# Block sums made in place for two weight matrices, norm sums in two row buffers, and one product moved, in a two-layer encoder step

## The chip, the cores and the metric

The kernel runs on one core of one Trainium2 chip. The metric is the device time of one execution in microseconds; three runs of the kernel before the change gave a median of 2988.94 us (2987.65 to 2989.17). PE is TensorE, DVE VectorE, ACT ScalarE, POOL GpSimd, SP the engine that issues the DMAs.

## The reference, cut to what matters

The step has two layers over 1024 prompt tokens and 8 x 16 sample tokens, 1152 columns in all, with 1024 features. Layer 0 mixes by forgetting attention, layer 1 by sliding-window attention. What the change touches is the part of each layer behind the attention:

```python
        h = h + _rms(mix, norm_mix_post[i])
        f = _swiglu(_rms(h, norm_ffn_pre[i]), ffn_w_gate[i], ffn_w_up[i], ffn_w_down[i])
        h = h + _rms(f, norm_ffn_post[i])
        gate = jax.nn.sigmoid(_rms(h, ple_norm[i]) @ ple_w_gate[i] + ple_b_gate[i])
        h = h + gate * (p[i] @ ple_w_proj[i])
```

with `_rms(x, g) = x * rsqrt(mean(x*x) + EPS) * g` over the features and `_swiglu(a, ...) = (silu(a @ w_gate) * (a @ w_up)) @ w_down`; the hidden width is 2816 = 22 x 128. All data are float32.

## The kernel before, in words

Activations lie with features on the partitions, in three column blocks of 384 columns: cC, cA and cB. A float32 product is made of three fp32r matmuls: each operand is split into a rounded high part (`round_r`, an ACT copy, L139) and the rest (`low_part`, a DVE subtraction, L145); `mm3` (L215 to L217) multiplies high by high, high by low and low by high.

`layer_tail` does everything behind the attention: output projection, residual and norms, SwiGLU, down projection, gate. Its steps are entered with `plan.add` and `plan.tile`; `Plan.run` then lists them: it keeps a planned clock for each of PE, ACT, DVE and LOAD (DMA issues on SP), takes at each turn the step that can start first (ties by due time), and calls it, so the order of the instructions on each engine is that in which the planner calls them. A step states its planned cost, the steps that it waits for, and which buffers it takes and frees; the dictionary in the `Plan(...)` call at L1085 says how many of each there are: one `acc`, two `sq`, two `y`, six product banks `mm`.

A norm (`plan_rms`, from L350) squares the eight feature tiles of a column block in four ACT activations of 768 columns. The first goes into `acc`, the others into `sq`; DVE adds them to `acc` (L365, 768 wide) and at last its two halves (L367). PE sums over the partitions (`total`, tile `pstat`, L233), DVE takes the root (`rsqrt`, 12 operations of 3 columns, L241 to L247), PE spreads it (`spread`, `prms`, L254), ACT copies it into a row `rr` (L380). For each block the output projection is followed by a norm, the residual (L424, L428; loads of the old h on SP, L420), a second norm and its gain products (`normed`, L1195).

The gate and up projections are computed by a Strassen-Winograd scheme on blocks: columns cA and cB against pairs of 128 hidden columns, feature halves against each other. The left operands are `Y11`, `Y21`, `Y22` and the differences `T1` to `T4` (`minus`, L1229, and `operand`, L139 and L145), made in the two `y` buffers which hold the mixer's blocks. The weight blocks are A and B, the two loaded 128x1024 pieces x1 and x2, and two sums, C and D, built on DVE by `s_sum` (L1315) from the halves X1 and X2 in a buffer of tag `y`. `matrix(g, up)` enters one weight matrix (11 groups g, gate and up): loads, splits (`parts_of`), seven half products of 12 matmuls into banks X, Y and Z, and the plain products of cC (`plain`, 24 matmuls, two halves). Bank X is used several times: Y11's product is copied out (`copied("11")`), T2 is added on top, copied (`"21"`, by ACT at L1353 for gate, by DVE at L1355 for up), then T1 is added on top, and so on. The first two matrices, (0, 0) and (0, 1), are `EARLY`: their plain products are made ahead (`when=0`), and they are loaded a second time for the Strassen products.

During the Strassen stage of layer 0 and 1 the weights of the gate stage are split as well (`presplit`, L1463 to L1478, through `st` and `sq`). The down projection (`kstep`) reads rows back from DRAM (`h_load`, L1529) and weights (`wd_load`, L1506).

Of the kernel before, what the change touches and what calls it, by code (L numbers as in the profile page):

```python
# [10 lines left out]
F32 = mybir.dt.float32  # L11
# [7 lines left out]
P = 128  # L19
D = 1024  # L20
KT = 8
# [67 lines left out]
def tile_kernel(ctx: ExitStack, tc: tile.TileContext, i, o, upto=99):  # L89
# [260 lines left out]
    def plan_rms(plan, src, after, out="rr", slot=None, ready=()):  # L350


        box = {}

        def square(k):
            if k:
                box[k] = t = tp.tile([P, 2, C], F32, name="sq", tag="sq", bufs=NSQ)
            else:
                box["acc"] = t = tp.tile([P, 2, C], F32, name="acc", tag="acc", bufs=1)
            nc.scalar.activation(t, src()[:, 2 * k:2 * k + 2, :], AF.Square)  # L360

        def gather(k):
            acc = box["acc"]
            if k < 4:
                nc.vector.tensor_tensor(acc, acc, box.pop(k), ADD)  # L365
            else:
                nc.vector.tensor_tensor(acc[:, 0], acc[:, 0], acc[:, 1], ADD)  # L367

        def sums():
            box["ps"] = total(box["acc"][:, 0])  # L370
# [11 lines left out]
        last = begin = plan.add(ACT, 0.735, step(square, 0), after[0], takes=["acc"])  # L382
        for k in range(1, 4):
            box["read"] = s = plan.add(ACT, 0.735, step(square, k), after[k] + [begin], takes=["sq"])
            last = plan.add(DVE, 0.87, step(gather, k), [s, last], frees=["sq"])
        last = plan.add(DVE, 0.47, step(gather, 4), [last])
# [679 lines left out]
    def layer_tail(l, oc, Wo, oa0, order, specs_kv=(), more=None):  # L1066
# [18 lines left out]
        plan = Plan(act=4 + (len(oa0[1]) == KT), raw=1, w0=2, w1=3, acc=1, sq=NSQ, rr=NRR, st=2, mm=6, hs=STB, row=NROW, y=2)  # L1085
# [204 lines left out]
        def matrix(g, up, when=1):  # L1290
# [58 lines left out]
            def copied(n, bank, eng=ACT):  # L1349

                def fn():
                    if eng == ACT:
                        nc.scalar.copy(put_row(temp(n)), ps(bank))  # L1353
                    else:
                        nc.vector.tensor_copy(put_row(temp(n)), ps(bank))  # L1355
                add(eng, 0.37 if eng == ACT else 0.47, fn, r=[(m, "ps", bank)], w=[(g, temp(n))], takes=["row"], **soon())
# [30 lines left out]

            whole = ("A", x1, [(m, "x", 0)]), ("B", x2, [(m, "x", 1)])
# [11 lines left out]
            wa = tags[m][0] if early else parts_of(m, *whole[0])  # L1400
            add(DVE, 0.6, step(s_sum, 1), r=[(m, "x", 1)], w=[(m, "s1")], takes=["y"])
# [6 lines left out]
            wb = tags[m][1] if early else parts_of(m, *whole[1])  # L1408
# [4 lines left out]
            if not early:  # L1413
                plain(0, "A", [])
                plain_out(0)
# [3 lines left out]
            product("X", "C", 1, "T2")  # L1419
            copied("21", "X", DVE if up else ACT)  # L1420
# [5 lines left out]
            if not early:  # L1426
                plain(1, "B", [])
                plain_out(1)
# [6 lines left out]
            if up:  # L1435
                diff("u11", "r12", "r11")
                store("r11", t_d[0, g], ("t", 0, g))
                diff("r12", "r22", "r12")
                diff("u22", "r22", "u11")
                store("u11", t_d[3, g], ("t", 3, g))  # L1440
                store("r22", t_d[2, g], ("t", 2, g))
                store("r12", t_d[5, g], ("t", 5, g))
                diff("u21", "r21", "u22")
                store("u22", t_d[4, g], ("t", 4, g))
                store("r21", t_d[1, g], ("t", 1, g))
                store("u21", t_d[6, g], ("t", 6, g))
# [61 lines left out]
        for half in range(2):  # L1508
            for f in range(FFT):
                last_load[0] = add(LOAD, 0.75, step(wd_load, f, half), w=[("W", f, half)], after=[last_load[0], marks[-2]],  # L1510
                                   takes=["act"] if half == 0 and f % 3 == 0 else [])

        def kstep(wsrc, wkey, hsrc, hkey, new, start, stop, evict):
# [24 lines left out]
            x = add(LOAD, 0.85, h_load, r=[hkey], after=last_row, takes=["row", "row"])  # L1538
# [708 lines left out]
```

## Time and profile before

| What | us |
|---|---|
| median of three runs | 2988.94 |
| the profiled execution | 2988.7 |
| its span | 2986.9 |
| PE busy in it | 2873.0 |
| DVE busy | 1894.1 |
| ACT busy | 1279.5 |

The span runs from the first to the last instruction on the chip; the execution's own time holds 1.8 us beside it. [...] A wait is given as the engine, the operation that waited, the one that released it, the total, how often, and the longest.

### The profile page before, as it was taken

The page shows a single profiled execution, that of the slowest core. Times are in us where ns is not written, and L with a number is a line of the kernel's source. Part 1 is how long each engine was busy: PE and PEld are TensorE (multiplying, and loading weights), DVE is VectorE, ACT ScalarE, POOL GpSimd, SP SyncE. Part 2 cuts the span into 40 slices and gives each one's busy share as a digit, 9 for nine tenths or more (in the row PEclk, how much of TensorE's full clock was granted, in tenths as well). Part 3 has the DMA queues.
Part 4 walks back from the last instruction along what each step waited for, and adds up shares of the span by engine and source line. Part 5 has one row for each costly group of instructions (what it writes and reads, how often), then busy time and mean ns, then how long its engine had stood idle before and what let it go on. Part 6 is the DMA issues. An engine that isn't in the chain of part 4 may idle for free. (4 is left out here: it accounts for less than half of the span.)

```text
span 2986.9 us, 48188 instructions
## 1 busy us (share of the span) xinstructions
PE 2873.0 (96%) x17564; PEld 2753.4 (92%) x17564; DVE 1894.1 (63%) x4187; ACT 1279.5 (43%) x2652; POOL 198.0 (7%) x324
## 2 busy tenths in 40 slices
PE   8999999998799999999999999998799999999999
PEld 8999877798699999999999988898799999999999
DVE  6253477767766656558878436658755555459875
ACT  6222266654433333345544245744433333255542
POOL 0000155400000000000000022200000000000000
PEclk9999999999799999999999999999899999999999
DMA  7364577534144444563365667344233333553364
GB/s 257 106 201 144 166 191 196 135 121 130 68 154 153 156 160 161 174 216 93 113 211 191 204 201 225 113 142 130 75 122 115 112 116 114 174 163 105 102 210 147
DMA packets 307041, 453.15 MB, mean 152 GB/s; under 512 B 40002, under 2 KB 253380, under 8 KB 306772
## 3 DMA queue, kind: packets, MB, share of 16 engines
q1 hardware_dynamic: 306804, 450.08, 47.9%
q8 instruction: 138, 2.26, 0.3%
q14 instruction: 99, 0.81, 0.1%
HBM read 315.60 MB, written 136.20 MB: 151 GB/s over the span
## 5 line engine op out<-in xcount | busy, mean ns | idle before, releaser
L215 PE MATMUL ps<-ahi,whi 128*128 128x384 f32 x1008 | 343.6, 341 | 0.7 <-ACT ev L589 0.7
L217 PE MATMUL ps<-ahi,wlo 128*128 128x384 f32 x1008 | 340.1, 337 | 0.2 <-DMA wlo<-wpg_d 0.2
L216 PE MATMUL ps<-alo,whi 128*128 128x384 f32 x1008 | 339.9, 337 | 0.0
L215 PE MATMUL pd<-row,whi 128*128 128x384 f32 x968 | 330.5, 341 | 9.5 <-ACT row L139 9.5
L216 PE MATMUL pd<-row,whi 128*128 128x384 f32 x968 | 329.8, 341 | 0.7 <-DVE row L145 0.7
L217 PE MATMUL pd<-row,wlo 128*128 128x384 f32 x968 | 328.5, 339 | 0.0
L215 PE MATMUL ps<-chi,whi 128*128 128x384 f32 x704 | 235.5, 335 | 0.0
L217 PE MATMUL ps<-chi,wlo 128*128 128x384 f32 x704 | 235.2, 334 | 0.0
L216 PE MATMUL ps<-clo,whi 128*128 128x384 f32 x704 | 235.2, 334 | 0.0
L145 DVE TENSOR_TENSOR wlo<-wraw,whi 128x1024 fp32r<-128x1024 f32 (+3 forms) x146 | 171.6, 1178 | 88.5 <-ACT whi L139 88.1
L139 ACT CAST whi<-wraw 128x1024 fp32r<-128x1024 f32 (+3 forms) x146 | 148.5, 1017 | 160.6 <-PE pX L216 58.3
L139 ACT CAST whi<-wd 128x512 fp32r<-128x512 f32 x198 | 122.4, 620 | 188.8 <-PE pd L216 165.6
L215 PEld LDWEIGHTS ps<-ahi,whi 128*128 128x128 f32 x1008 | 191.8, 190 | 6.2 <-issue 4.9
L145 DVE TENSOR_TENSOR wlo<-wd,whi 128x512 fp32r<-128x512 f32 x198 | 135.8, 688 | 95.2 <-ACT whi L139 93.5
L215 PEld LDWEIGHTS pd<-row,whi 128*128 128x128 f32 x968 | 183.3, 189 | 11.9 <-ACT row L139 10.8
L217 PEld LDWEIGHTS ps<-ahi,wlo 128*128 128x128 f32 x1008 | 191.4, 190 | 0.7 <-DMA wlo<-wpg_d 0.5
L216 PEld LDWEIGHTS ps<-alo,whi 128*128 128x128 f32 x1008 | 191.7, 190 | 0.0
L216 PEld LDWEIGHTS pd<-row,whi 128*128 128x128 f32 x968 | 183.2, 189 | 1.8 <-DVE row L145 1.8
L217 PEld LDWEIGHTS pd<-row,wlo 128*128 128x128 f32 x968 | 183.0, 189 | 0.0
L215 PE MATMUL pX<-T,whi 128*128 128x384 f32 x352 | 120.6, 342 | 37.6 <-ACT whi L139 28.7
L139 ACT CAST whi<-y 128x1024 fp32r<-128x1024 f32 x88 | 92.7, 1053 | 124.4 <-DVE y L1315 62.7
L1353 ACT COPY row<-pX 128x384 f32<-128x384 f32 x110 | 52.5, 477 | 218.0 <-PE pX L217 216.7
(273 smaller groups left out, 7244.2 us busy)
## 6 DMA issues: line engine op xcount, KB each, us to landing
t_d<-row SPq DMA_DIRECT2D x154, 192.0 KB
row<-t_d SPq DMA_DIRECT2D x154, 192.0 KB
wraw<-in_w_gate SPq DMA_DIRECT2D x48, 512.0 KB
wraw<-in_w_up SPq DMA_DIRECT2D x48, 512.0 KB
wd<-in_w_down SPq DMA_DIRECT2D x88, 256.0 KB
row<-hc_d SPq DMA_DIRECT2D x88, 192.0 KB
wpg_d<-sq SPq DMA_DIRECT2D x64, 256.0 KB
st<-h_d SPq DMA_DIRECT2D x72, 192.0 KB
```

The costliest lines, as they stand in the source:

```text
L139: return nc.scalar.copy(out, in_)
L145: return nc.vector.tensor_tensor(out, x, hi.bitcast(F32), SUB)
L215: nc.tensor.matmul(ps, w[0], a[0], start=first, stop=False, skip_group_check=more)
L216: nc.tensor.matmul(ps, w[0], a[1], start=False, stop=False, skip_group_check=more)
L217: nc.tensor.matmul(ps, w[1], a[0], start=False, stop=last, skip_group_check=more)
L1353: nc.scalar.copy(put_row(temp(n)), ps(bank))
```

## The change

The change has four parts. In `plan_rms` every square goes into a `sq` buffer, `acc` is one row of 384 columns, of which there are two (`acc=2`), and the additions are all 384 wide: seven in place of three of 768 and one of 384. For the two early matrices `s_sum` is replaced by `in_raw`, which writes the four block sums into the halves of the loaded weights themselves; C is then raws 0 and D raws 1, with another assignment of halves to products, and no `y` buffer is taken. In the other matrices the product of A with Y21 (bank Z) stands behind the one of C with T2 and the copy "21", and that copy is always ACT's. Last, the planned costs of `wd_load` and `h_load` are 0.9 and 0.7 in place of 0.75 and 0.85.

```diff
         def square(k):
-            if k:
-                box[k] = t = tp.tile([P, 2, C], F32, name="sq", tag="sq", bufs=NSQ)
+            box[k] = t = tp.tile([P, 2, C], F32, name="sq", tag="sq", bufs=NSQ)
+            nc.scalar.activation(t, src()[:, 2 * k:2 * k + 2, :], AF.Square)
+
+        def gather(k, half):
+            t = box[k]
+            if k == 0:
+                box["acc"] = acc = tp.tile([P, C], F32, name="acc", tag="acc", bufs=2)
+                nc.vector.tensor_tensor(acc, t[:, 0], t[:, 1], ADD)
             else:
-                box["acc"] = t = tp.tile([P, 2, C], F32, name="acc", tag="acc", bufs=1)
...
+                nc.vector.tensor_tensor(box["acc"], box["acc"], t[:, half], ADD)
...
-        plan = Plan(act=4 + (len(oa0[1]) == KT), raw=1, w0=2, w1=3, acc=1, sq=NSQ, rr=NRR, st=2, mm=6, hs=STB, row=NROW, y=2)
+        plan = Plan(act=4 + (len(oa0[1]) == KT), raw=1, w0=2, w1=3, acc=2, sq=NSQ, rr=NRR, st=2, mm=6, hs=STB, row=NROW, y=2)
...
+            if early:
+
+                def in_raw(x, xs, a_, as_, b_, bs, op):
+                    add(DVE, 0.6, lambda: nc.vector.tensor_tensor(raws[m, x][:, xs], raws[m, a_][:, as_], raws[m, b_][:, bs], op),
+                        r=[(m, "x", a_), (m, "x", b_)], w=[(m, "x", x)])
+
+                in_raw(1, X2, 1, X1, 1, X2, ADD)
+                in_raw(1, X1, 0, X1, 1, X1, SUB)
+                in_raw(0, X1, 1, X2, 0, X1, SUB)
+                in_raw(0, X2, 0, X2, 0, X1, SUB)
+                wc = parts_of(m, "C", x1, [(m, "x", 0)])
+                wd = parts_of(m, "D", x2, [(m, "x", 1)])
+                wb = tags[m][1]
+                unload()
+                product("X", "A", 0, "Y11", new=True)
+                copied("11", "X")
+                product("Z", "A", 1, "Y21", new=True, frees=[wa])
+                added("11", "Z", ["mm"])
+                final("11")
+                product("X", "C", 0, "T2")
+                copied("21", "X")
+                product("Y", "D", 0, "T3", new=True)
+                product("X", "D", 1, "T1", frees=[wd])
...
             product("X", "A", 0, "Y11", new=True)
             copied("11", "X")
-            if not early:
-                plain(0, "A", [])
-                plain_out(0)
-            product("Z", "A", 1, "Y21", new=True, frees=[wa])
-            added("11", "Z", ["mm"])
-            final("11")
-            product("X", "C", 1, "T2")
-            copied("21", "X", DVE if up else ACT)
+            plain(0, "A", [])
+            plain_out(0)
+            product("X", "C", 1, "T2")
+            copied("21", "X")
+            product("Z", "A", 1, "Y21", new=True, frees=[wa])
+            added("11", "Z", ["mm"])
+            final("11")
             product("Y", "D", 0, "T3", new=True)
...
-                last_load[0] = add(LOAD, 0.75, step(wd_load, f, half), w=[("W", f, half)], after=[last_load[0], marks[-2]],
+                last_load[0] = add(LOAD, 0.9, step(wd_load, f, half), w=[("W", f, half)], after=[last_load[0], marks[-2]],
...
-            x = add(LOAD, 0.85, h_load, r=[hkey], after=last_row, takes=["row", "row"])
+            x = add(LOAD, 0.7, h_load, r=[hkey], after=last_row, takes=["row", "row"])
```

On DVE, at the first Strassen matrix of layer 0, before the change: y_8622 is the buffer of the gate matrix's sums, wraw its loaded weights, wlo the low parts of C and D, T2 to T4 the operands.

```order
L145 TENSOR_TENSOR T2_8592<-y_7975,T2_8592 128x384 x4
L145 TENSOR_TENSOR T3_8580<-y_7975,T3_8580 128x384 x4
L145 TENSOR_TENSOR T1_8544<-y_7627,T1_8544 128x384 x4
L1229 TENSOR_TENSOR y_7627<-y_7627,y_7975 128x384 x4
L145 TENSOR_TENSOR T4_8613<-y_7627,T4_8613 128x384 x2
L1315 TENSOR_TENSOR y_8622<-wraw_8257 128x512
L145 TENSOR_TENSOR T4_8613<-y_7627,T4_8613 128x384
L1315 TENSOR_TENSOR y_8622<-y_8622,wraw_8254 128x512
L1315 TENSOR_TENSOR y_8622<-wraw_8254,wraw_8257 128x512
L1315 TENSOR_TENSOR y_8622<-wraw_8254,y_8622 128x512
L145 TENSOR_TENSOR T4_8613<-y_7627,T4_8613 128x384
L145 TENSOR_TENSOR wlo_8628<-y_8622,whi_8627 128x1024
```

After the change the same place is in two pieces; first the norms' part, where L1411 is `in_raw` and L1194 the gain product of cB (y_8002):

```order
L145 TENSOR_TENSOR Y21_8389<-y_7634,Y21_8389 128x384
L1411 TENSOR_TENSOR wraw_8299<-wraw_8299 128x512
L145 TENSOR_TENSOR wlo_8544<-wraw_8346,whi_8543 128x1024
L1194 SCALAR_TENSOR_TENSOR y_8002<-y_8002,gains_103,rr_8592 128x384
L145 TENSOR_TENSOR wlo_8596<-wraw_8299,whi_8595 128x1024
```

and, some rows further on, the operands:

```order
L1228 TENSOR_TENSOR y_8002<-y_8002 128x384 x3
L1228 TENSOR_TENSOR y_8002<-y_8002,y_7634 128x384 x4
L145 TENSOR_TENSOR T2_8640<-y_8002,T2_8640 128x384 x4
L145 TENSOR_TENSOR T3_8626<-y_8002,T3_8626 128x384 x4
L1368 TENSOR_TENSOR row_8373<-row_8373,ps_8429 128x384
L145 TENSOR_TENSOR T1_8607<-y_7634,T1_8607 128x384 x4
```

The block sums and the two low parts have moved from behind the operands T2, T3 and T1 to a place ahead of cB's gain products.

On PE, ahead of the first Strassen product of layer 0: chi and clo are the split cC of a plain block, pstat and prms a norm's sums and its spread root. Before:

```order
L217 MATMUL ps_8391<-chi_7897,wlo_8236 128x384
L233 MATMUL pstat_8433<-ones_68,acc_8308 128x1 x3
L254 MATMUL prms_8463<-ident_104,ry_8444 128x128 x3
L233 MATMUL pstat_8482<-ones_68,acc_8440 128x1 x3
L254 MATMUL prms_8506<-ident_104,ry_8491 128x128 x3
L215 MATMUL pX_8521<-Y11_8476,whi_8071 128x384
```

After:

```order
L217 MATMUL ps_8493<-chi_7903,wlo_8316 128x384
L233 MATMUL pstat_8552<-ones_68,acc_8491 128x1 x3
L254 MATMUL prms_8574<-ident_104,ry_8560 128x128 x3
L215 MATMUL pZ_8579<-Y21_8389,whi_8097 128x384
L216 MATMUL pZ_8579<-Y21_8389,whi_8097 128x384
```

Before, two norms lie between the last plain block and Y11's product. Now one lies there, in front of Y21's product; the other one and Y11's product have moved ahead of that plain block.

On PE, in a later matrix (2, 0) of layer 0, the end of the first plain block and what follows it; pZ is A's product with Y21, pX bank X with C's product with T2. Before:

```order
L216 MATMUL ps_9292<-clo_7898,whi_9047 128x384
L217 MATMUL ps_9292<-chi_7897,wlo_9048 128x384
L215 MATMUL pZ_9343<-Y21_8511,whi_9047 128x384
L216 MATMUL pZ_9343<-Y21_8511,whi_9047 128x384
L217 MATMUL pZ_9343<-Y21_8511,wlo_9048 128x384
```

After:

```order
L216 MATMUL ps_9326<-clo_7904,whi_9081 128x384
L217 MATMUL ps_9326<-chi_7903,wlo_9082 128x384
L215 MATMUL pX_9303<-T2_8640,whi_9100 128x384
L216 MATMUL pX_9303<-T2_8640,whi_9100 128x384
L217 MATMUL pX_9303<-T2_8640,wlo_9101 128x384
```

T2's product into bank X and Y21's into bank Z have changed places.

## Rows read from the trace of the kernel before

**Rows 1.** The page, busy time of each engine, share of the span, instructions.

```profile
PE 2873.0 (96%) x17564; PEld 2753.4 (92%) x17564; DVE 1894.1 (63%) x4187; ACT 1279.5 (43%) x2652; POOL 198.0 (7%) x324
```

**Rows 2.** PE's waits over the whole span: total us, times, longest us.

```profile
PE pX L215 <- ACT whi L139: 28.7, 2, 14.3
PE pstat L233 <- DVE acc L367: 17.0, 7, 4.0
...
PE pd L215 <- ACT row L139: 9.5, 4, 4.1
PE pX L215 <- DVE row L1355: 8.8, 8, 1.8
```

**Rows 3.** Windows: length, busy us of each engine (x instructions), PEclk, DMA share, GB/s.

```profile
720.00:740.00 20.00, 14.80 (x89) 14.09 (x88) 17.70 (x48) 7.81 (x12) 0.00 (x0) 0.96 0.45 142
740.00:760.00 20.00, 9.79 (x32) 9.25 (x33) 19.55 (x48) 9.68 (x20) 0.00 (x0) 0.59 0.08 26
760.00:780.00 20.00, 4.94 (x15) 3.93 (x15) 18.45 (x36) 7.86 (x14) 0.00 (x0) 0.50 0.15 52
780.00:800.00 20.00, 19.43 (x104) 19.11 (x103) 13.15 (x18) 7.91 (x11) 0.00 (x0) 0.93 0.27 90
1541.40:1565.40 24.00, 24.00 (x139) 23.71 (x137) 11.03 (x21) 6.98 (x12) 0.00 (x0) 1.00 0.97 339
1569.40:1574.60 5.20, 5.20 (x17) 5.20 (x17) 4.28 (x17) 3.66 (x5) 0.00 (x0) 0.50 0.22 66
```

**Rows 4.** DVE's timeline, layer 0: start us, us, line, operation, xcount.

```profile
722.74 3.07 DVE L365 TENSOR_TENSOR acc<-acc,sq 128x768 f32<-128x768 f32 x3
...
733.59 0.55 DVE L367 TENSOR_TENSOR acc<-acc 128x384 f32<-128x384 f32 x1
...
735.66 0.15 DVE L241 TENSOR_SCALAR rv<-pstat 128x3 f32<-128x3 f32 x1
...
737.91 0.95 DVE L365 TENSOR_TENSOR acc<-acc,sq 128x768 f32<-128x768 f32 x1
...
749.42 2.73 DVE L1195 SCALAR_TENSOR_TENSOR y<-y,gains,rr 128x384 f32<-128x384 f32 x5
...
763.57 5.70 DVE L145 TENSOR_TENSOR T<-y,T 128x384 fp32r<-128x384 f32 x12
...
772.01 0.67 DVE L1315 TENSOR_TENSOR y<-wraw 128x512 f32<-128x512 f32 x1
...
775.36 2.34 DVE L145 TENSOR_TENSOR wlo<-y,whi 128x1024 fp32r<-128x1024 f32 x2
```

**Rows 5.** PE's timeline, layer 0, with the idle time before and its releaser.

```profile
774.88 0.69 PE L215 MATMUL pX<-T,whi 128*128 128x384 f32 x1 [14.33 <-ACT whi L139]
...
776.62 0.69 PE L217 MATMUL pX<-T,wlo 128*128 128x384 f32 x1 [0.72 <-DVE wlo L145]
...
786.21 0.45 PE L215 MATMUL pX<-Y,whi 128*128 128x384 f32 x1 [0.57 <-ACT row L1353]
```

**Rows 6.** Groups by form: xcount, busy us, mean ns, idle us before, releasers.

```profile
L365 DVE TENSOR_TENSOR acc<-acc,sq 128x768 f32<-128x768 f32 x90 | 85.7, 953 | 35.1 <-ACT sq L360 34.0
...
L1353 ACT COPY row<-pX 128x384 f32<-128x384 f32 x110 | 52.5, 477 | 218.0 <-PE pX L217 216.7 <-DMA t_d<-row 1.2
...
L1355 DVE COPY row<-pX 128x384 f32<-128x384 f32 x22 | 12.1, 550 | 0.0
```

**Rows 7.** Timelines of DVE and PE in a later matrix of layer 0.

```profile
924.02 1.22 DVE L145 TENSOR_TENSOR wlo<-y,whi 128x1024 fp32r<-128x1024 f32 x1
...
954.49 0.33 PE L215 MATMUL pX<-T,whi 128*128 128x384 f32 x1
```

**Rows 8.** PE's timeline in the gate stage, layer 0 and layer 1.

```profile
1568.08 0.77 PE L233 MATMUL pstat<-ones,acc 128*128 128x1 f32 x3 [2.64 <-DVE acc L367]
...
2898.60 0.58 PE L233 MATMUL pstat<-ones,acc 128*128 128x1 f32 x4 [3.40 <-DVE acc L367]
```

**Rows 9.** SP's DMA issues ahead of the down projection, layer 0.

```profile
1258.64 9.37 SPq L1506 DMA_DIRECT2D wd<-in_w_down  x13
```

More of the change, by code (lines that the diff above doesn't have):

```diff
@@ L355, in square @@
         def square(k):
[L356 to L367 removed]
+            box[k] = t = tp.tile([P, 2, C], F32, name="sq", tag="sq", bufs=NSQ)
[5 more added lines that the diff above has]
+                nc.vector.tensor_tensor(acc, t[:, 0], t[:, 1], ADD)
+            else:
+                nc.vector.tensor_tensor(box["acc"], box["acc"], t[:, half], ADD)
         def sums():
[L370 removed]
+            box["ps"] = total(box["acc"])
         def root():
@@ L380, in copy @@
             nc.scalar.copy(r, box["pr"][:, :C])
[L382 to L386, printed above, removed]
+        s = last = None
+        for k in range(4):
+            box["read"] = s = plan.add(ACT, 0.735, step(square, k), after[k] + [s], takes=["sq"] if k else ["sq", "acc"])
+            if k:
+                last = plan.add(DVE, 0.47, step(gather, k, 0), [s, last])
+            last = plan.add(DVE, 0.47, step(gather, k, 1), [s, last], frees=["sq"])
         last = plan.add(PE, 0.65, sums, [last], takes=["st"], frees=["acc"], first=True)
@@ L1347, in matrix, with copied @@
             temp = ("u" if up else "r").__add__
[L1349 to L1356, printed above, removed]
+            def copied(n, bank):
+                add(ACT, 0.37, lambda: nc.scalar.copy(put_row(temp(n)), ps(bank)), r=[(m, "ps", bank)], w=[(g, temp(n))], takes=["row"], **soon())
             def added(n, bank, frees):
@@ L1386, in diff, with combined @@
                 add(DVE, 0.47, lambda: nc.vector.tensor_tensor(R(out_), R(x), R(y_), SUB), r=[(g, x), (g, y_)], w=[(g, out_)], **soon(3.0))
+            def combined():
+                diff("u11", "r12", "r11")
+                store("r11", t_d[0, g], ("t", 0, g))
+                diff("r12", "r22", "r12")
+                diff("u22", "r22", "u11")
+                store("u11", t_d[3, g], ("t", 3, g))
+                store("r22", t_d[2, g], ("t", 2, g))
+                store("r12", t_d[5, g], ("t", 5, g))
+                diff("u21", "r21", "u22")
+                store("u22", t_d[4, g], ("t", 4, g))
+                store("r21", t_d[1, g], ("t", 1, g))
+                store("u21", t_d[6, g], ("t", 6, g))
             whole = ("A", x1, [(m, "x", 0)]), ("B", x2, [(m, "x", 1)])
@@ L1400, in matrix @@
             wa = tags[m][0] if early else parts_of(m, *whole[0])
+            if early:
[19 more added lines that the diff above has]
+                product("X", "D", 1, "T1", frees=[wd])
+                copied("22", "X")
+                added("22", "Y", [])
+                final("22")
+                product("X", "C", 1, "Y22", frees=[wc])
+                direct("r12", lambda: ps("X"), (m, "ps", "X"))
+                product("Y", "B", 1, "T4", frees=[wb])
+                added("21", "Y", ["mm"])
+                final("21")
+                marks.append(plan.tiles[-1])
+                if up:
+                    combined()
+                return
             add(DVE, 0.6, step(s_sum, 1), r=[(m, "x", 1)], w=[(m, "s1")], takes=["y"])
@@ L1407, in matrix @@
             release(["y"], [(m, f"s{n}") for n in range(1, 5)])
-            wb = tags[m][1] if early else parts_of(m, *whole[1])
+            wb = parts_of(m, *whole[1])
             unload()
@@ L1425, in matrix @@
             final("22")
-            if not early:
-                plain(1, "B", [])
-                plain_out(1)
+            plain(1, "B", [])
+            plain_out(1)
             product("X", "D", 1, "Y22", frees=[wd])
@@ L1435, in matrix @@
             if up:
[L1436 to L1446, printed above, removed]
+                combined()
         tags = {}
```

## The prediction

> **What bounds the kernel now.** I read the page's busy line first: PE is busy in 96% of the span, DVE in 63%, ACT in 43% [rows 1]. So time can only come from PE's pauses and from stretches in which PE's clock is low. PE's waits were read next [rows 2]: the two longest are for a rounded weight of the first Strassen matrix, 14.3 us in each layer, then the norms' column sums (17.0 in 7), the split rows of the down projection (9.5 in 4) and the product bank that DVE copies at L1355 (8.8 in 8). Then the stretch around the first 14.3 us wait, in windows of 20 us [rows 3]: 240 matmuls are done in 80 us. At full pace 139 take 24.00 us (1541.4 to 1565.4), 0.173 each, so 240 are worth 41.5 us: some 38.5 us are lost there, once per layer. In the two middle windows DVE is busy for 19.55 and 18.45 of 20 us, the granted clock is 0.59 and 0.50: PE stands, the DVE chain sets the end.
>
> What this chain is, the DVE timeline shows [rows 4]. The last norm sums of column block cA stand behind cB's residual (722.74 and 733.59), its root follows at 735.66, the gain products come later, and the T splits run from 763.57. T2 is the first of the three in that row of twelve: 5.70 / 12 = 0.475 us each, so it is ready at 763.57 + 1.9 = 765.5. PE starts the T2 product at 774.88 [rows 5], 9.4 us later, since the weight C is missing: its block sums start at 772.01, and its low split runs from 775.36. The sums wait for a buffer of tag y, and both hold the mixer's output until the last T operand is formed.
>
> **The change part by part.**
>
> Block sums in the loaded weights. For the first two matrices the four sums write into the raw weights and take no y buffer. In the DVE order shown with the change, the gate matrix's sums and the two splits of C and D now stand before T2, between the norms' operations. The wait for C goes; what is late next is T2 itself. I work out its time on DVE. Without any shift it is ready at 765.5. Put in front of it are four sums of 0.67 us and two splits of 2.34 together [rows 4]: 4 x 0.67 + 2.34 = 5.0 us. If nothing else moved, T2 would be ready at 770.5; the gain per layer is then 774.9 - 770.5 = 4.4. That is the poor end.
>
> Norm sums in two rows of buffers. With acc = 2 the second norm of cA no longer waits until cB's first norm gives the single buffer back; the order has its sums, its root and seven of its eight gain products before cB's residual (I count the five that stand before cB's root, since the others fall where DVE waits), and Y11's product before the last plain block, where PE still has work. What leaves the stretch: sums 3.07 + 0.55, root 737.91 - 735.66 = 2.25, five products 2.73, together 8.6 us [rows 4]. Each norm has seven half-wide additions in place of three wide and one half-wide: by starts 7 x 0.47 against 3 x 0.87 + 0.47, 0.2 us more on DVE. (0.47 is what twelve splits of the same width take each, 0.475; 0.87 is the 0.95 of L365 [rows 6] less the same 0.08 of overlap.) T2 is then ready at 765.5 + 5.0 - 8.6 + 0.2 = 762.1. The other end: if the sums and splits fall wholly into gaps where DVE waits for PE's norm matmuls, 757. I take 762, and with it a gain of 12.9 per layer; the 0.72 for the low part of C [rows 5] goes as well, and I leave it as a margin for queues. Two layers: 26, ends 9 and 36. The pace after the wait is taken as before.
>
> One product moved, the u21 copy put on ACT. In the twenty later matrices per layer the T2 product follows the plain block, and Y21's product stands behind it, so that two products lie between T2 and the next use of bank X instead of one. A product has 12 matmuls, 12 x 0.173 = 2.08 us; the copy's cover grows to 4.16. The 8.8 us behind L1355, at most 1.8 each [rows 2], go. Price of the other side: the first copy (Y11) loses Z's 2.08 us and has the plain block alone, up to 4.16 us, against 0.48 us of copy on ACT [rows 6]. The T2 product's own weight C is ready long before: in a later matrix its low split ended at 925.24 for a product that starts at 954.49 [rows 7], 29 us ahead, so coming 2.08 us earlier costs nothing; without that lead it would cost these 2.08 per matrix. The 22 copies leave DVE (22 x 0.55 = 12.1) and come to ACT (22 x 0.48 = 10.5), which is busy 43%. ACT's instructions run in the program's order, and in layer 0 casts of the gate stage's weights stand ahead of some copies; ends are 8.8 gained and 8 lost, I take 8 gained, near the row of the wait.
>
> Norms elsewhere. There are 30 norms, 30 x 0.2 = 6 us on DVE, hidden wherever PE has work; without that cover it would be 0.2 on a chain per norm. In the gate stage after the down projection the new order has cA's first norm 152 matmuls earlier, as it needs no buffer of cB's; cB's second norm, which waits there now, stays where it was, with two shorter additions at its end (0.5 us less). PE waits for it for 2.64 and 3.40 us [rows 8], and pays for the first again with a low clock: 17 matmuls in 5.20 us instead of 2.9 [rows 3]. So up to some 11 us could go in both layers (the waits and twice 2.3 and more for the clock); or, if the residual's loads from DRAM end last, these waits stay and the earlier norm adds one of 2.6 in each. Ends -11 and +5, I take -3, nearer to the waits that stay.
>
> Costs of two loads in the planner (0.9 and 0.7). The first row of the down projection is issued before 18 loads of weights are out instead of 21. Thirteen such issues took 9.37 us [rows 9], 0.72 each: 2.2 us earlier, of a first wait of at most 4.1. The second row is behind 22 and gets no sooner. I take 0, ends -4 and +4.
>
> Sum: 26 + 8 + 3 = 37. The profiled execution took 2988.7 (span 2986.9, 1.8 outside), 0.2 below the median shown, so no shift: 2988.7 - 37 = 2952.
>
> [...] DVE stood idle for 35.1 us in all ahead of norm sums, nearly all of it for ACT's squares, while what came later in its order waited too [rows 6]. [...]
>
> [...]
>
> **Rivals.**
> 1. The operands end last anyway: sums and splits stand in front of T2 and the norms' shift gains nothing. For it: DVE is full there. Against: 8.6 us leave the stretch. Gain 2 x 4.4 + 8 = 17, the norms' 3 aside: 2972.
> 2. The clock stays high through the shorter pauses. T2 to T1 lose less: 774.88 to 786.21 with 0.72 and 0.57 of waits is about 10 us for 36 matmuls, 6.2 at full pace, 3.8 per layer: 2952 - 8 = 2944. Against: even 2.64 us of waiting [rows 8] was followed by 0.50 [rows 3].
> 3. Slower: bank X is now reused with only the plain block behind the first copy, and ACT has every copy in its queue behind casts that wait for a PE product or a transfer. With 40 later matrices it outweighs the 29 us of the other terms once more than 0.73 us is lost in each; at 1.6, a cast and a half, 64 are lost: 2988.7 - 29 + 64 = 3024. Against: ACT's copies spent 216.7 us waiting for PE [rows 6], so most run at once.
> 4. The change does not do what it says: the gate weights' second load lands late, the sums come no earlier than now, and C ends last again. For it: that load waits for a raw buffer that the up matrix's split frees. Against: it has until the residual is done. Only 8 + 3 is left: 2978.
>
> **How the numbers follow.** Forecast 0.60, rival 1 0.13, rival 2 0.13, rival 3 0.04, rival 4 0.10. The terms' ends add to 2929 (36 + 8.8 + 11 + 4 gained) and 2997 (9 gained, 8 + 5 + 4 lost), but not all go one way; the forecast's own range is 2941 to 2963. With rivals 1 and 2 taken in: 2936 to 2973; outside are part of 4 and all of 3. Within 0.2% is within 6 us of before, about what this measurement can tell from none. Faster 0.92, same 0.04, slower 0.04.
>
> **What would show it.** In the new profile the wait of the bank X product for ACT's weight rounding in the first matrix should be gone, and a wait for T2's split of some 10 to 13 us stand in its place, with the T2 product starting about 13 us sooner in each layer. The 20 us window with clock 0.50 should shrink. The waits after L1355 should be gone, with none above 1 us behind the ACT copies. Wrong would be: the same 14 us wait, T2's product 5 us earlier or less, new waits of bank X in the later matrices, or larger ones for the column sums in the gate stage.

## The result, and the profile after

The changed kernel takes 2956.8 us in the median of four runs (2953.5 to 2960.8) beside 2989.1 of the kernel before (2987.7 to 2990.6): ratio 0.9892, 95% interval 0.9875 to 0.991. The forecast was 2952, with 2941 to 2963 as its own range. The sum was nearly met, but not by the terms that it was made of: the largest was 9 us too high, the rest together 7.5 too low.

The page of the profiled execution (2953.5 us, span 2951.7) answers to [rows 1]:

```profile
PE 2867.3 (97%) x17564; PEld 2750.6 (93%) x17564; DVE 1892.2 (64%) x4255; ACT 1289.8 (44%) x2674; POOL 197.4 (7%) x324
```

PE's waits over the whole span of the changed kernel, as in [rows 2]:

```profile
PE pstat L233 <- DVE acc L365: 21.7, 8, 4.7
PE pX L215 <- ACT T L139: 19.1, 2, 9.7
...
PE pd L215 <- ACT row L139: 6.4, 6, 1.7
PE prms L254 <- DVE ry L247: 5.0, 2, 2.5
PE pd L216 <- DVE row L145: 4.5, 6, 1.3
```

The two waits of 14.3 for the rounded weight are gone, and in their place stand two of 9.4 and 9.7 for the operand T2 (`ACT T`). No wait behind a copy of bank X above 0.6 us is left. The column sums (`pstat`) wait longer than before, 21.7 in place of 17.0: that is the line which the prediction did not have.

The four windows of [rows 3], now with 340 matmuls in 80 us in place of 240. PEclk is the clock granted to PE as a share of its full one; at 1.00 a matmul of the first row below has 20.00 / 122 = 0.16 us of busy time, at 0.65 one of the second 8.19 / 33 = 0.25, so in these rows the number of matmuls tells PE's pace and its busy share does not:

```profile
720.00:740.00 20.00, 20.00 (x122) 19.92 (x121) 18.16 (x44) 11.06 (x19) 0.00 (x0) 1.00 0.34 111
740.00:760.00 20.00, 8.19 (x33) 7.33 (x32) 19.43 (x45) 7.92 (x13) 0.00 (x0) 0.65 0.39 127
760.00:780.00 20.00, 14.21 (x67) 13.49 (x68) 19.90 (x41) 10.36 (x21) 0.00 (x0) 0.76 0.06 21
780.00:800.00 20.00, 20.00 (x118) 20.00 (x117) 17.72 (x26) 8.25 (x12) 0.00 (x0) 1.00 0.51 168
```

DVE is as full as before (18.16 to 19.90 of 20 us in the first three). Where time came from is read best from a few instructions that both programs have. PE's timeline of the kernel before; S is a product of layer 0's attention, pT a transpose at the end of layer 1's, the last row the T2 product of layer 1:

```profile
590.70 0.62 PE L967 MATMUL S<-qk 128*128 128x384 f32 x2 [1.00 <-DVE mn L972]
...
1948.92 0.76 PE L1999 MATMUL pT<-ident,tt 128*128 128x128 f32 x5 [0.82 <-POOL tt L1994]
...
2114.07 0.69 PE L215 MATMUL pX<-T,whi 128*128 128x384 f32 x1 [14.33 <-ACT whi L139]
```

The same of the changed kernel, with the column sums that wait, the T2 products (764.58 and 2083.71) and Y22's product (774.57), which follows T2's, T3's and T1's; it answers to [rows 5] and [rows 8]:

```profile
589.20 0.62 PE L966 MATMUL S<-qk 128*128 128x384 f32 x2 [1.00 <-DVE mn L971]
...
671.33 1.41 PE L233 MATMUL pstat<-ones,acc 128*128 128x1 f32 x6 [3.21 <-DVE acc L365]
...
746.52 1.41 PE L233 MATMUL pstat<-ones,acc 128*128 128x1 f32 x6 [4.46 <-DVE acc L365]
...
764.58 0.69 PE L215 MATMUL pX<-T,whi 128*128 128x384 f32 x1 [9.41 <-ACT T L139]
...
774.57 0.45 PE L215 MATMUL pX<-Y,whi 128*128 128x384 f32 x1 [0.57 <-ACT row L1350]
...
1548.43 1.41 PE L233 MATMUL pstat<-ones,acc 128*128 128x1 f32 x6 [3.02 <-DVE acc L365]
...
1926.41 0.77 PE L2029 MATMUL pT<-ident,tt 128*128 128x128 f32 x5 [0.81 <-POOL tt L2024]
...
1988.57 0.80 PE L233 MATMUL pstat<-ones,acc 128*128 128x1 f32 x6 [1.80 <-DVE acc L365]
...
2032.61 1.37 PE L233 MATMUL pstat<-ones,acc 128*128 128x1 f32 x6 [2.20 <-DVE acc L365]
...
2083.71 0.69 PE L215 MATMUL pX<-T,whi 128*128 128x384 f32 x1 [9.67 <-ACT T L139]
...
2867.65 0.80 PE L233 MATMUL pstat<-ones,acc 128*128 128x1 f32 x6 [1.56 <-DVE acc L365]
```

The differences of these starts, with [rows 5] and [rows 8] for before, make a ledger of the 35.2 us between the two spans:

| Stretch | before | after | difference |
|---|---|---|---|
| start to S, layer 0 | 590.70 | 589.20 | -1.5 |
| S to T2's product, layer 0 | 184.18 | 175.38 | -8.8 |
| T2's product to the gate stage's column sum | 793.20 | 783.85 | -9.4 |
| from there to pT, layer 1 | 380.84 | 377.98 | -2.9 |
| pT to T2's product, layer 1 | 165.15 | 157.30 | -7.9 |
| T2's product to the gate stage's column sum | 784.53 | 783.94 | -0.6 |
| from there to the end of the span | 88.3 | 84.05 | -4.2 |

The gate stage's column sum in this table is the one that waits; it is another norm's in the two programs, but it stands behind the same number of products. The first row is scatter: over all kernels of this document S starts between 589.2 and 593.5.

T2's product comes 8.8 and 7.9 us sooner, not 12.9. The moved product's stage shows 9.4 in layer 0 and nothing in layer 1. New are the waits of column sums at 671.33, 1988.57 and 2032.61, in the output projection, where no wait of PE was listed before, and a short one of 0.80 at 716.85. The first one in windows of 20 us; before, then after:

```profile
660.00:680.00 20.00, 19.90 (x118) 19.57 (x117) 13.32 (x32) 6.49 (x11) 0.00 (x0) 1.00 0.50 160
```

```profile
660.00:680.00 20.00, 16.79 (x83) 16.46 (x82) 9.00 (x26) 4.08 (x7) 0.00 (x0) 0.83 0.46 147
```

35 matmuls fewer, at 0.173 us each 6 us, for a wait listed as 3.21: the granted clock fell to 0.83 as well. What was late, DVE's timeline of the changed kernel shows:

```profile
663.64 0.56 DVE L427 TENSOR_TENSOR mix<-mix,st 128x384 f32<-128x384 f32 x1 [2.71 <-DMA st<-in_xT]
...
670.03 1.15 DVE L365 TENSOR_TENSOR acc<-acc,sq 128x384 f32<-128x384 f32 x2 [0.50 <-ACT sq L357]
```

The residual waits 2.71 us for its old h from DRAM, and the last addition of the norm ends at 671.18. PE reaches the column sum at 671.33 - 3.21 = 668.12. In the kernel before, the last addition (L367, 0.56 us from 671.10) ended 80.96 us behind S; now it ends 81.98 behind S, so the cheaper additions made nothing sooner here. The planner, with 0.47 us for each narrow addition and 0.55 for a load, put the column sum 12 matmuls further ahead on PE than before, and everything behind it waited. The next column sum, which does not wait and stands behind the same matmuls, starts 106.9 us behind S (696.14) where it was 101.0 (691.66).

### The profile page after: what moved, and what is told of

It is laid out like the page before. It is cut to its first block, busy times and chain, and to the rows that moved or that the text cites. A ratio compares the mean times of both kernels' runs of the same rounds, so it can differ in the third digit from the quotient of the medians.

```text
span 2951.7 us, 48321 instructions
## 1 busy us (share of the span) xinstructions
PE 2867.3 (97%) x17564; PEld 2750.6 (93%) x17564; DVE 1892.2 (64%) x4255; ACT 1289.8 (44%) x2674; POOL 197.4 (7%) x324
## 5 line engine op out<-in xcount | busy, mean ns | idle before, releaser
L145 DVE TENSOR_TENSOR wlo<-wraw,whi 128x1024 fp32r<-128x1024 f32 (+3 forms) x154 | 181.4, 1180 | 79.6 <-ACT whi L139 79.4
L139 ACT CAST whi<-wraw 128x1024 fp32r<-128x1024 f32 (+3 forms) x154 | 156.9, 1019 | 160.9 <-PE pX L216 58.9
L1350 ACT COPY row<-pX 128x384 f32<-128x384 f32 x132 | 63.1, 478 | 207.4 <-PE pX L217 204.8
L2024 POOL TENSOR_SCALAR tt<-tt,l 128x256 f32<-128x256 f32 (+1 forms) x128 | 59.6, 484 | 1258.8 <-DMA r<-r_d 1117.5
```

The costliest lines, as they stand in the source:

```text
L139: return nc.scalar.copy(out, in_)
L145: return nc.vector.tensor_tensor(out, x, hi.bitcast(F32), SUB)
L1350: add(ACT, 0.37, lambda: nc.scalar.copy(put_row(temp(n)), ps(bank)), r=[(m, "ps", bank)], w=[(g, temp(n))], takes=["row"], **soon())
L2024: nc.gpsimd.tensor_scalar(tt[:, g, :nw], tt[:, g, :nw], l[:, g:g + 1], 1.0, op0=MULT, op1=MULT)
```

## The experiments

My theory after these readings was that the early block sums and the norms' buffers are two chains on DVE, one behind the other; the rivals were that one of them gains nothing. The distance from S (layer 0) and from pT (layer 1) to T2's product, each from the run's PE timeline as above, is the measure for it:

| Kernel | median us | ratio to before (95%) | S to T2 | pT to T2 |
|---|---|---|---|---|
| before | 2989 | | 184.18 | 165.15 |
| changed | 2956.8 | 0.9892 (0.9875 to 0.991) | 175.38 | 157.30 |
| 1 early sums alone | 2971.4 | 0.9934 (0.992 to 0.9949) | 175.24 | 156.53 |
| 2 norms alone | 2988.0 | 0.9991 (0.998 to 1.0002) | 188.80 | 165.27 |
| 3 product and copy alone | 2978.3 | 0.9955 (0.9938 to 0.9972) | 184.18 | 165.31 |
| 4 load costs alone | 2986.6 | 0.9989 (0.9976 to 1.0001) | 184.20 | 165.18 |
| 5 changed, old norms | 2959.9 | 0.9897 (0.9883 to 0.9911) | 176.17 | 156.89 |
| 6 changed, later column sums | 2945.8 | 0.9857 (0.9843 to 0.987) | 167.76 | 149.61 |
| 7 changed, old product order | 2972.2 | 0.9947 (0.9935 to 0.996) | 174.47 | 156.91 |
| 8 changed, old load costs | 2954.4 | 0.9882 (0.9869 to 0.9895) | 177.06 | 154.36 |
| 9 the copy alone | 2979.2 | 0.9967 (0.9956 to 0.9979) | 183.81 | 165.37 |
| 10 the product alone | 2978.6 | 0.9968 (0.9957 to 0.9978) | 183.86 | 165.22 |
| 11 norms, later column sums | 2974.1 | 0.9952 (0.9939 to 0.9964) | 179.18 | 161.36 |
| 12 changed, still later | 2946.3 | 0.9862 (0.9849 to 0.9876) | 170.18 | 151.60 |

Each distance comes from one execution. The kernel before, 3, 4, 9 and 10 are the same program up to these products, and agree within 0.4 us. The changed kernel, 7 and 8 are the same up to there as well, and differ by 2.6 and 2.9: behind the column sums that wait the granted clock is not the same (in the 20 us from 660 it is 0.83 with 83 matmuls in the changed kernel, 0.91 with 93 in 7). Between kernels with such waits, differences below 3 us are not read as effects.

**1. The early sums alone.** The early branch with `in_raw`, with the old norms, product order and costs.

```diff
+            if early:
+                in_raw(1, X2, 1, X1, 1, X2, ADD)
...
+                wc = parts_of(m, "C", x1, [(m, "x", 0)])
+                wd = parts_of(m, "D", x2, [(m, "x", 1)])
```

> The kernel before with the block sums of the two early matrices made in the loaded weights, and nothing else of the change (one acc, old products, old costs). Theory A (the wait for C and the late second norm are two chains one behind the other on DVE; both have to go): the 14.33 us wait for the rounded weight goes, but the sums stand ahead of cB's residual and the norms are where they were, so T2 is the prediction's poor end: some 4.4 us sooner per layer, 2989 - 9 = 2980, with a wait of about 10 us for T's split. Theory B (the sums alone are the gain, the norms' buffers add nothing): T2 8 to 9 us sooner per layer as in the whole change, 2989 - 17 = 2972. Theory C (they are made early but hold up the residual): no gain or slower, 2989 or more.

18 us, theory B: the sums alone bring T2 forward by 8.9 and 8.6 us, as much as the whole change. PE's timeline of this kernel:

```profile
593.51 0.62 PE L967 MATMUL S<-qk 128*128 128x384 f32 x2 [1.01 <-DVE mn L972]
...
768.75 0.69 PE L215 MATMUL pX<-T,whi 128*128 128x384 f32 x1 [2.28 <-ACT T L139]
```

and its DVE, at the sums, their splits and the first T split:

```profile
721.66 2.14 DVE L1417 TENSOR_TENSOR wraw<-wraw 128x512 f32<-128x512 f32 x3 [0.16 <-DMA wraw<-in_w_gate]
...
726.83 0.69 DVE L1417 TENSOR_TENSOR wraw<-wraw 128x512 f32<-128x512 f32 x1
...
728.30 1.22 DVE L145 TENSOR_TENSOR wlo<-wraw,whi 128x1024 fp32r<-128x1024 f32 x1
...
740.45 1.22 DVE L145 TENSOR_TENSOR wlo<-wraw,whi 128x1024 fp32r<-128x1024 f32 x1
...
769.48 1.02 DVE L145 TENSOR_TENSOR T<-y,T 128x384 fp32r<-128x384 f32 x2
```

The T splits start 769.48 - 593.51 = 175.97 behind S; before it was 763.57 - 590.70 = 172.87 [rows 4]. So of the 5.0 us of sums and splits 3.1 lengthened the chain and 1.9 did not: DVE's pauses on the way are some 1.0 us shorter, and an addition of a result row (0.55) now comes behind the T splits; the rest is not accounted for. And the product starts 0.73 before the first T split: it needs only the high part, which ACT makes.

**2. The norms alone.** `plan_rms` as changed and `acc=2`, nothing else.

```diff
-        plan = Plan(... acc=1, ...)
+        plan = Plan(... acc=2, ...)
```

> The kernel before with the norm sums in two one-row buffers, seven half-wide additions, and nothing else of the change. Theory A: C is still formed behind the T operands, but the whole DVE chain up to it is shorter by the norm of cA that has moved ahead; the wait for the rounded weight stays, several us shorter than 14.33, T2 5 to 8 us sooner per layer less 3 to 4 us for the new waits of column sums in the output projection (3.21 in layer 0, 1.80 and 2.20 in layer 1 of the changed kernel): 2989 - 8 = 2981, between 2975 and 2987. Theory B (C ends last whatever the norms do): 2989. Theory C (the new column-sum waits are a net cost): 2992 to 2996.

Same time as before: no part of theory A's 5 to 8 us is left. The number is theory B's; its reason is not, as experiment 11 shows. T2 is 4.6 later in layer 0 and where it was in layer 1. Its PE timeline has the wait in the output projection too:

```profile
671.58 1.41 PE L233 MATMUL pstat<-ones,acc 128*128 128x1 f32 x6 [2.91 <-DVE acc L365]
...
778.52 0.69 PE L215 MATMUL pX<-T,whi 128*128 128x384 f32 x1 [24.29 <-ACT whi L139]
```

The difference between the layers goes with the granted clock, 0.83 and 0.91 in the windows of layer 0, 1.00 in those of layer 1. The windows of the output projection in which PE waits, first layer 0, then layer 1; below them the kernel before (its first window is shown above):

```profile
660.00:680.00 20.00, 17.09 (x84) 16.75 (x84) 9.55 (x27) 3.75 (x6) 0.00 (x0) 0.83 0.49 155
710.00:730.00 20.00, 18.73 (x104) 18.40 (x103) 17.37 (x40) 10.24 (x16) 0.00 (x0) 0.91 0.55 171
2005.00:2025.00 20.00, 17.63 (x106) 17.30 (x105) 13.07 (x34) 7.19 (x13) 0.00 (x0) 1.00 0.40 130
2050.00:2070.00 20.00, 18.24 (x111) 17.91 (x110) 18.65 (x49) 11.44 (x18) 0.00 (x0) 1.00 0.51 162
```

```profile
710.00:730.00 20.00, 20.00 (x121) 19.96 (x120) 13.76 (x29) 10.72 (x16) 0.00 (x0) 1.00 0.36 126
2005.00:2025.00 20.00, 20.00 (x120) 19.96 (x119) 14.48 (x34) 9.01 (x17) 0.00 (x0) 1.00 0.28 90
2050.00:2070.00 20.00, 20.00 (x120) 19.96 (x119) 14.50 (x30) 9.99 (x15) 0.00 (x0) 1.00 0.38 129
```

In layer 0, 34 and 17 matmuls fewer are done, 51 x 0.173 = 8.8 us; in layer 1, at a full clock, 14 and 9 fewer, 4.0 us. The two differ by 4.8, T2's shifts by 4.5.

**3. Product and copy alone.** The later matrices as changed.

```diff
-            copied("21", "X", DVE if up else ACT)
+            copied("21", "X")
             product("Z", "A", 1, "Y21", new=True, frees=[wa])
```

> The kernel before with only the product order of the later matrices changed (T2's product behind the plain block, Y21's behind its copy) and all copies of bank X on ACT. Theory A: the eight waits behind L1355, all in layer 0 and 8.8 us together, go with the clock never having fallen there, and layer 1, which had none, gains nothing: 2989 - 8.8 = 2980. Theory B (the waits come back behind the ACT copies): 2989 or more. Theory C (the order also speeds the start of the stage): below 2977.

Theory A, with 11 us. In the 450 us from 800 of layer 0 the kernel before and this one, in windows:

```profile
800.00:1250.00 450.00, 441.11 (x2532) 438.24 (x2531) 276.56 (x477) 155.83 (x265) 0.00 (x0) 1.00 0.48 155
```

```profile
800.00:1250.00 450.00, 450.00 (x2598) 450.00 (x2598) 274.49 (x472) 162.30 (x279) 0.00 (x0) 1.00 0.50 158
```

66 matmuls more, 66 x 0.173 = 11.4 us, at a granted clock of 1.00 in both. In layer 1 nothing changed, since there no such wait had been.

**4. The load costs alone.**

```diff
-  add(LOAD, 0.75, step(wd_load, f, half), ...)
+  add(LOAD, 0.9, step(wd_load, f, half), ...)
```

(and `h_load` 0.85 to 0.7)

> The kernel before with only the planned costs of the two loads changed (0.9 and 0.7). Theory A: the down projection's first rows come a little sooner or later, -1 to +2 us: 2988 to 2991. Theory B (part of the gain is from here: its row waits were 3.45 and 4.07 and are 0.99 to 1.74 in the changed kernel): 2989 - 6 = 2983.

2.8 us less, between the two theories, but the interval holds 1. With experiment 8 it is no effect that can be measured.

**5. The change with the old norms.**

```diff
-        plan = Plan(... acc=2, ...)
+        plan = Plan(... acc=1, ...)
```

(and the old `square`, `gather` and their steps)

> The changed kernel with the old norm (one acc, three wide additions and a half-wide one); early sums, moved product and load costs as changed. Theory A (the norms' buffers gain nothing: what they take out of the DVE chain ahead of T2 they give back in the output projection, where a column sum now comes too early): 2989 - 18 - 11 - 3 = 2957, the same as the changed kernel's 2957, with the column-sum wait of 3.21 us in the output projection gone and T2 at the same distance from the attention. Theory B (both chains must go, as predicted): T2 about 8 us later in each layer than in the changed kernel, 2957 + 16 = 2973. Theory C (the norms cost): 2951 to 2954.

Theory A: 2959.9 with an interval that covers the changed kernel's. In the changed kernel the norms' part gave nothing that can be measured.

**6. The change with later column sums.** No operation differs, only the planned cost of a norm's last addition, and with it the order on every engine.

```diff
-            last = plan.add(DVE, 0.47, step(gather, k, 1), [s, last], frees=["sq"])
+            last = plan.add(DVE, getattr(plan, "pad", 0.47) if k == 3 else 0.47, step(gather, k, 1), [s, last], frees=["sq"])
...
+        plan.pad = 0.85
```

> The changed kernel with the planned cost of each norm's last addition in the part behind the attention at 0.85 in place of 0.47; no operation differs, only the planned order (the first two column sums behind the output projection stand 12 matmuls later on PE). Theory A (the norms' gain is there and is lost to a column sum placed too early: in the 20 us from 660 the changed kernel does 83 matmuls where the kernel before does 118, 35 x 0.173 = 6 us): the wait of 3.21 shrinks to about 1 and with it the low clock, and T2 comes 3 to 5 us sooner in each layer: 2957 - 8 = 2949. Theory B (T2 is set by DVE's own work, whatever PE does): 2957. Theory C (the wait only moves to the next column sum): 2957, with that wait up by as much.

Theory A, and more at T2 than expected: 7.6 and 7.7 us sooner than in the changed kernel. It is faster than both kernels; its interval lies below the changed kernel's. Its window of the output projection and its T2 product:

```profile
660.00:680.00 20.00, 20.00 (x120) 19.75 (x119) 13.82 (x36) 6.88 (x12) 0.00 (x0) 1.00 0.54 174
```

```profile
591.35 0.61 PE L966 MATMUL S<-qk 128*128 128x384 f32 x2 [1.01 <-DVE mn L971]
...
759.11 0.69 PE L215 MATMUL pX<-T,whi 128*128 128x384 f32 x1 [8.81 <-ACT T L139]
```

120 matmuls, clock 1.00, no wait. But T2's gain is not all kept. In the new order the low parts of C and D stand behind T2's splits on DVE and no longer ahead of them; PE starts T2's product and then waits for C's low part:

```profile
762.99 0.69 PE L217 MATMUL pX<-T,wlo 128*128 128x384 f32 x1 [1.85 <-DVE wlo L145]
...
772.23 0.45 PE L215 MATMUL pX<-Y,whi 128*128 128x384 f32 x1 [0.57 <-ACT row L1351]
```

From T2's product to Y22's it takes 13.1 and 12.3 us, in the changed kernel 10.0 and 10.8. So Y22's product is 4.5 and 6.3 us sooner, 10.8 together, and by 11.0 the medians differ. Against experiment 5, which has the old norms, T2 is 8.4 and 7.3 us sooner and Y22's product some 6 in each layer: what the norms are worth once their column sums don't hold PE.

**7. The change with the old product order and DVE's copy.**

```diff
             product("Z", "A", 1, "Y21", new=True, frees=[wa])
...
-            copied("21", "X")
+            copied("21", "X", DVE if up else ACT)
```

> The changed kernel with the old product order in the later matrices and the copy of the up matrices on DVE again. Theory A (the parts add): 2957 + 11 = 2968, with some eight waits behind L1355 of about 9 us together in layer 0. Theory B (the other parts have already shifted the stage so that these waits don't come back): 2957 to 2960.

Theory A or a little more: 15 us slower than the changed kernel, with nine waits behind DVE's copy.

```profile
PE pX L215 <- DVE row L1354: 9.9, 9, 1.6
```

**8. The change with the old load costs.**

```diff
-  add(LOAD, 0.9, step(wd_load, f, half), ...)
+  add(LOAD, 0.75, step(wd_load, f, half), ...)
```

> The changed kernel with the old planned costs of the two loads (0.75 and 0.85). Theory A (as the small difference of the costs alone): 2957 + 3 = 2960, with the first wait of the down projection at 3 to 5 us again in place of several of about 1 us. Theory B: no difference, 2957.

Theory B: the interval covers the changed kernel's ratio. Its first wait of the down projection is 4.45, as theory A had it, but the several short ones that it replaces are as long together: 10.6 in 4, against 6.4 and 4.5 in the changed kernel.

**9 and 10. The two halves of the moved product.** First only the copy on ACT, with the old order; then only the order, with the copy on DVE.

```diff
-            copied("21", "X", DVE if up else ACT)
+            copied("21", "X")
```

> The kernel before with only the copy "21" of the up matrices on ACT in place of DVE; the order of the products is the old one, T3's product alone (2.08 us) between T2's and T1's. In the kernel before, DVE's copy came late since DVE had waited 3.87 us for a transfer of the gate stage's weights and had a split of 1.22 to do. Theory A (the engine of the copy is the cause: ACT has the copy at once, 0.48 us against 2.08 of cover): all waits go, 2989 - 11 = 2978 as with both halves. Theory B (the distance between the products is the cause): waits come back behind ACT, 2984 to 2989.

```diff
-            product("Z", "A", 1, "Y21", new=True, frees=[wa])
...
             copied("21", "X", DVE if up else ACT)
+            product("Z", "A", 1, "Y21", new=True, frees=[wa])
```

> The kernel before with only Y21's product moved behind T2's and its copy, so that two products (4.16 us) lie between T2's and T1's; the copy of the up matrices stays on DVE. Theory A (the engine is the cause, but the longest wait listed was 1.8 and the cover grows by 2.08): all or nearly all waits go here too, 2978 to 2981, each half of the edit being enough. Theory B (only the engine counts): 2986 to 2989, with waits behind DVE's copy left.

Theory A in both: 11 us each, the same as together. With the copy on ACT no wait behind it is left in these matrices; with the order alone one is:

```profile
PE pX L215 <- DVE row L1355: 0.9, 1, 0.9
```

Each half is enough, the other adds nothing that can be measured.

**11. The norms with later column sums, sums as before.** The kernel of experiment 2 with the edit of 6.

```diff
+        plan.pad = 0.85
```

> The kernel before with the norm sums in two one-row buffers and the planned cost of the last addition at 0.85, so that the column sums behind the output projection stand 12 matmuls later; the block sums are made behind the T operands as before. Theory A (the norms' gain of some 8 us per layer is separate from that of the early sums; an early column sum alone had eaten it): the column-sum wait of 2.91 at 671 us goes and T2 comes about 7 us sooner than in the run of the norms alone in each layer, still behind the rounded weight: 2988 - 14 = 2974. Theory B (the sums behind T4 end last whatever the norms do): 2985 to 2989.

Theory A's time: 14 us less than experiment 2. T2 is 9.6 and 3.9 us sooner and not 7 in each layer, since experiment 2 had lost more in layer 0; against the kernel before T2 is 5.0 and 3.8 sooner, with C still the operand that ends last.

**12. Still later column sums.** Experiment 6 with 1.5 in place of 0.85.

```diff
-        plan.pad = 0.85
+        plan.pad = 1.5
```

> The changed kernel with the planned cost of each norm's last addition behind the attention at 1.5: the column sums stand 12 to 36 matmuls later than in the changed kernel, 0 to 24 later than with 0.85. Theory A (with 0.85 no matmul in the output projection waits any more, so what is left ahead of T2 is DVE's own chain, and pushing the sums further back only delays the roots): 2946 or a few us more. Theory B (the remaining column-sum waits of 4.7 and 5.3 us are of the same kind and shrink): 2938 to 2942.

Theory A: no more to gain, and T2 2.4 and 2.0 us later than with 0.85. The column sum of cB still waits, 6.33 us. The row names ACT's `Y`, but DVE's last addition for this norm, in the second fence, ends at 742.13, 0.14 us ahead of the column sum; in experiment 6, where the row names `acc`, that distance is 0.15 (741.52 and 741.67). So it waits for its own additions, as there, and it comes as far behind S as there (150.21 and 150.32): T2's 2.4 us arise behind it.

```profile
742.27 1.41 PE L233 MATMUL pstat<-ones,acc 128*128 128x1 f32 x6 [6.33 <-ACT Y L139]
```

```profile
741.58 0.55 DVE L365 TENSOR_TENSOR acc<-acc,sq 128x384 f32<-128x384 f32 x1
```

## Why the prediction was right, and where it was not

**Block sums early: the forecast's small part, worth twice as much.** It gave 4.4 us per layer if nothing else moved; experiment 1 measured 8.9 and 8.6. The working is repaired by two terms. T2 "ready at 763.57 + 1.9" counted all four low splits, but PE starts with the high part, 0.7 us before the first split: 2.6 us. And of the 5.0 us put in front 1.9 did not lengthen the chain. 4.4 + 2.6 + 1.9 = 8.9.

**Norm sums in two buffers: the step that failed.** "What leaves the stretch: ... together 8.6 us" was taken as a gain at T2. The work does leave the stretch, but its new place was not followed to the end: with the single buffer gone and cheaper additions the planner also placed column sums earlier on PE in the output projection, and there PE stood for 3.21 us and lost 6. That put the next column block's norm, and with it the whole chain to T2, back by what had been won (experiments 2 and 5). Of the 8.4 that the prediction worked out (8.6 less 0.2) some 6 are there as soon as those column sums stand later (Y22's product, 5 against 6), and 5.0 and 3.8 where the block sums are not early (T2's, before against 11). The edit of 6 and 11 moves other operations too, the low parts of C and D among them, but the loss that it takes away is seen on PE ahead of T2's stretch: the third column sum of the output projection starts 106.9 us behind S in the changed kernel, 101.0 in the kernel before and 100.8 in experiment 6 (692.11). The step followed the moved work on DVE, in T2's stretch, and not on PE, in the stage ahead of it. PE's matmuls start in the order of the program in the profiles of both kernels (17564 in each), and in the 20 us around one column sum that waits 35 matmuls of the output projection fewer are done.

So the term of 26 was 8.8 + 7.9 = 16.7, by other parts than it was made of. That the whole came within 5 us of the forecast is luck: the rest of the ledger gives 18.5 where 8 + 3 = 11 were taken.

**Moved product and copy: right, sized too low.** 8 were taken, near the row of the wait; 11 alone and 15 when undone were measured, and the matmul counts of experiment 3 give 11.4. The cause lies in how a wait is listed. At 1124.85 of the kernel before, PE's first matmul behind a wait follows the one ahead of it by 2.10 us, and the wait is listed with 1.75 (rows below); at full pace the distance is 0.173, so 1.93 are lost, and the next one follows by 0.28, another 0.11.

```profile
1122.75 0.34 PE L217 MATMUL pY<-T,wlo 128*128 128x384 f32 x1
1124.85 0.44 PE L215 MATMUL pX<-T,whi 128*128 128x384 f32 x1 [1.75 <-DVE row L1355]
1125.13 0.34 PE L216 MATMUL pX<-T,whi 128*128 128x384 f32 x1
```

0.29 us more than listed, eight times 2.3: 8.8 + 2.3 = 11.1. Behind each of the other seven the next start follows by 0.28 as well. For the nine waits of experiment 7 the same gives 9.9 + 2.6 = 12.5 of its 15 us. The wait is listed from the end of the row ahead of it, 1123.09, which is 0.34 behind that row's start, though matmuls of its kind follow each other by 0.173. Why the copy was late is in the trace as well: on DVE, whose 4187 instructions start in the program's order in this profile (as ACT's 2358 do, accumulator reads and table loads aside), it stood behind a wait of 3.87 us for a transfer of the gate stage's weights (to 1121.37) and a split of 1.22 (at 1123.11), so putting it on another engine or further from its reader does equally (9 and 10). The prediction spoke of twenty matrices in each layer; all eight waits were in layer 0.

**Norms elsewhere.** 3 were taken. In the kernel with the norms alone the stretches outside S to T2 and pT to T2 sum to 4.5 us less than before, of which 1.0 lies ahead of S: the size fits, as far as single executions tell. In layer 0 the gate stage's column sum waits as long as before (3.02 against 2.64), as it was taken; in layer 1 it waits less (1.56 against 3.40).

**Load costs.** 0 was taken: right (4 and 8). But time moves: in the changed kernel the first matmul of layer 0's down projection comes 477.6 us behind Y22's product, with the old costs (8) 481.0, and from its first to its last matmul the projection takes 268.0, with the old costs 264.1.

**Rivals.** The first, that operands end last anyway, is what the two long waits are now, and its price for the norms (nothing) was right, for another reason than the one it gave. The second fell short: the clock in the two windows is 0.65 and 0.76 where it was 0.59 and 0.50, but behind the wait T2's matmuls still follow each other by 0.32 us in place of 0.173 (10 distances in layer 0 and 15 in layer 1, before 17 and 14), and T2's product to Y22's takes 9.99 us in place of 11.33 in layer 0 and 10.84 in place of 10.77 in layer 1, where it asked for 3.8 less in each. The third and the fourth did not come: no wait behind ACT's copies above 0.6, and the sums run ahead of T2.

**What stays open.** Why the granted clock fell behind the column sums of layer 0 in experiment 2 and not behind those of layer 1 is not shown. Whether the 8.8 us that PE still waits for T2 in experiment 6 can be shortened was not tried; experiment 12 shows only that later column sums don't do it.

## What to carry to other kernels

When a list scheduler orders the program, a buffer more or a cheaper step moves work on every engine, and the gain is real only if no other engine is brought to a place where its operand isn't there yet: look for new waits in the stages ahead of the one that was to gain, and correct the planned cost, not the work. A forecast whose total comes true can be wrong in each term; running each part alone and the whole without it costs little and shows it. Where a waiting engine is fed by two others, ask which of its operands it needs for its first instruction, not for its last.

## What was not expected of the hardware

The eight waits of PE behind L1355 cost some 0.3 us each more than the profile lists, at an unchanged clock of 1.00 (8.8 us listed, 66 matmuls or 11.4 us lost). A longer one cost more still: 3.21 us listed took 35 matmuls, 6 us, with the clock at 0.83 in that window. The length alone does not tell the clock here: a wait of 2.37 us (experiment 2, 2005 to 2025) left 1.00, one of 2.20 us (changed kernel, 2025 to 2045) left 0.83. On DVE the halved additions take 116 us in all (210 of 0.55) where the wide ones and the last had taken 102 (85.7 [rows 6] and 30 of 0.55), and yet the kernel with the old ones (5) is no faster. DVE waits 28.8 us in all for ACT's squares among the new ones.
